# A mixer in two phases: input projection of the first 1024 tokens by seven block products, all recurrent chains after it

## The chip, the cores and the metric

The kernel runs on one core of a Trainium2 chip. Its time is the device time of one execution in microseconds; of several runs the median stands. PE is the matrix engine, DVE the vector engine, ACT the scalar engine, POOL the engine called GpSimd, SP the engine that issues most DMAs. DMAs run beside all of them.

## The reference

One layer over 2048 tokens of 1024 features, in fp32:

```
mod = silu(c) @ w_ada + b_ada             # six vectors: shift, scale, gate of mixer and feed-forward
p   = adaln(x, shift_m, scale_m) @ w_in   # 1024 -> 3592: gate_b, gate_c, h_conv, q, k, v, z, a, bt
ya  = rms_norm(gate_b * conv3(gate_c * h_conv))            # 512 wide, groups of 64
q, k, v = silu(conv4(q, k, v)); q, k normalized            # 4 heads of 128
o   = gated delta rule(q, k, v, g(a), beta(bt))            # a state per head, carried from token to token
yb  = rms_norm(o) * silu(z)
x   = x + gate_m * (concat(ya, yb) @ w_out)
x   = x + gate_f * ((silu(h @ w_gate) * (h @ w_up)) @ w_down)   # h = adaln(x, shift_f, scale_f)
out = adaln(x, shift_o, scale_o)
```

The delta rule goes in chunks: within a chunk a triangular system is solved; between chunks a state of 128 by 128 per head is carried, so chunk j+1 cannot begin before chunk j has updated the state. The convolutions are causal, three or four taps along the tokens.

## The kernel before

Dense products are made in fp32 accuracy from three matmuls: every operand is cut in a high part (a rounding on ACT, L389 for weights) and a low part (a difference on DVE, L391), and high times high, high times low and low times high are added in PSUM (`dmm`, L322).

The mixer takes the tokens in four blocks of 512. For each block the normalized rows are transposed to feature-major, scaled, shifted and split (`hTh`, `hTl`). Then 28 strips of 128 columns of w_in follow, 8 x 3 = 24 matmuls each: k, q, v and z of four heads, then four times gate_c, h_conv and gate_b. Sixteen narrow matmuls give a and bt. Behind each k, q and v strip stands its convolution on DVE (L1246, L1248) and a SiLU on ACT. Last comes the output projection, 8 strips of w_out, 192 matmuls for a block, whose result times gate_m is added to x and written to DRAM (`x1d`).

Beside the strips run the chains of the same block, written as generators: `head_chain` (decay and beta, the kk products, the triangular solve of diagonal pieces on DVE, L1041 and L1043, with a trip over DRAM before L1058), `level_chain` (products that join the pieces, L1082 to L1117), `q_chain`, `v_chain`, `chunk_chain` (L1182 to L1213: four matmul groups a chunk, each with a DVE step behind it), `out_chain` (norm, transposes at L1231, the pieces of yb at L1238) and `mix_chain` (the branch ya, with a reciprocal of 128x512 on DVE at L1321). A yield names what the next piece waits for. Every third dense matmul calls `tick`, which lets those generators go on whose next piece a planner (`Clock`, with estimated costs) holds to be ready. The order on PE, DVE, ACT and POOL is then fixed as the planner saw it. Each engine works through its list in that order.

Work in the background (`bg`) advances one step with each strip's weights: sums over w_ada (`mod_gen`), eight steps of 128x1024 on DVE at L469 for each vector; gate_m in block 0, the two vectors of the feed-forward norm in block 1, gate_f in block 2. The norm of x before the feed-forward (`second_norm`) runs one block behind. The feed-forward comes after and uses seven block products already.

## Time and profile before

| what | value |
|---|---|
| time, median of 3 runs | 2402.55 us (2399.51 to 2403.01) |
| the profiled execution | 2403.85 us, span 2402.1 us |
| PE / DVE / ACT / POOL busy | 2341.1 / 1788.3 / 1051.7 / 571.4 us |
| mixer (until the last output matmuls) | about 0 to 1055 us |
| DMA, mean over the span | 142 GB/s |

The page's parts are read in this order: busy shares and the 40 slices, then the chain that ended last, then windows over the mixer's stages, and last the chain of waits in one block with DVE's order of time beside it. Where PE's list holds a row that waits for another engine, everything behind it on PE waits too, even if it is ready.

### The profile page before, as it was taken

How to read it: one execution, taken by the hardware profiler on the slowest of the kernel's cores; microseconds unless marked ns; L12 is line 12 of the kernel's file. 1: busy time of each engine (PE TensorE's matmuls, PEld its weight loads, DVE VectorE, ACT ScalarE, POOL GpSimd, SP SyncE). 2: the span in 40 equal slices, each digit the busy share in tenths (PEclk: the TensorE clock that was granted, in tenths of full speed). 3: DMA queues.
4: the chain of work that ended last, by engine and by line, in shares of the span. 5: the costliest groups of instructions: out<-in, count | busy, mean ns of one | idle time of the engine just before them, and what ended most of it. 6: DMA issues, size and time to landing. Idle time of an engine off the chain costs nothing.

```text
span 2402.1 us, 31013 instructions
## 1 busy us (share of the span) xinstructions
PE 2341.1 (97%) x11317; PEld 1939.5 (81%) x11317; DVE 1788.3 (74%) x2673; ACT 1051.7 (44%) x1790; POOL 571.4 (24%) x643
## 2 busy tenths in 40 slices
PE   6999999999999999999999999999999999999998
PEld 5788888887888788887778888878888877887786
DVE  5988889775987678787556556875656569878888
ACT  3644664344544473366433334433333323322345
POOL 0340344033513161211000000000000036434447
PEclk9999999999999999999999999999999999999999
DMA  7443565535463445156664334753433374333433
GB/s 252 123 118 89 171 189 165 147 106 166 136 167 115 126 135 145 47 168 174 209 185 119 101 106 117 251 162 88 128 97 110 101 241 163 106 123 119 136 129 151
DMA packets 401136, 341.20 MB, mean 142 GB/s; under 512 B 39811, under 2 KB 343180, under 8 KB 400918
## 3 DMA queue, kind: packets, MB, share of 16 engines
q1 hardware_dynamic: 399430, 336.75, 45.9%
q0 software_dynamic: 1152, 2.10, 0.6%
q8 instruction: 89, 1.46, 0.2%
q14 instruction: 65, 0.53, 0.1%
q10 hardware_dynamic: 400, 0.36, 0.0%
HBM read 265.74 MB, written 75.51 MB: 142 GB/s over the span
## 4 chain that ended last, share of the span: by engine, by line
PE 66%; DVE 16%; DMA 7%; ACT 4%; issue 4%; POOL 2%; SPq 0%; ACTq 0%; DVEq 0%; POOLq 0%
PE pd L322 41%; PE pm L322 17%; DVE wlo L391 3%; DVE cv L1248 2%; DVE acc L1822 1%; DMA wraw<-in_w_in_dram 1%; ACT whi L389 1%; DMA y<-xT 1%; DVE wraw L469 1%; POOL wraw L1751 1%; DVE cv L1246 1%; PE pm L1082 1%; DMA A12d<-y 1%; DMA acc<-x 1%; PE pm L1090 1%
## 5 line engine op out<-in xcount | busy, mean ns | idle before, releaser
L389 ACT CAST whi<-wraw 128x1024 fp32r<-128x1024 f32 x286 | 299.7, 1050 | 404.5 <-PE pd L322 174.5
L391 DVE TENSOR_TENSOR wlo<-wraw,whi 128x1024 fp32r<-128x1024 f32 x286 | 361.9, 1266 | 98.4 <-ACT whi L389 94.2
L322 PE MATMUL pd<-hTh,whi 128*128 128x512 f32 x888 | 359.3, 406 | 0.6 <-ACT hTh L573 0.6
L322 PE MATMUL pd<-hTl,whi 128*128 128x512 f32 x888 | 346.9, 391 | 0.6 <-DVE hTl L574 0.6
L322 PE MATMUL pd<-hTh,wlo 128*128 128x512 f32 x888 | 347.2, 391 | 0.0
L322 PEld LDWEIGHTS pd<-hTh,wlo 128*128 128x128 f32 x888 | 166.8, 188 | 36.5 <-issue 0.3
L322 PEld LDWEIGHTS pd<-hTh,whi 128*128 128x128 f32 x888 | 167.3, 188 | 32.2 <-ACT hTh L573 1.0
L322 PEld LDWEIGHTS pd<-hTl,whi 128*128 128x128 f32 x888 | 167.6, 189 | 30.9 <-DVE hTl L574 1.1
L1616 POOL TENSOR_TENSOR wraw<-wraw 128x1024 f32<-128x1024 f32 x2 | 4.9, 2466 | 782.2 <-DMA wraw<-in_w_down_dram 773.8
L1564 DVE TENSOR_TENSOR sg<-sg,pd 128x512 f32<-128x512 f32 x44 | 30.2, 686 | 169.8 <-PE pd L322 169.8
L1822 DVE TENSOR_TENSOR acc<-acc,pd 128x512 f32<-128x512 f32 x192 | 127.4, 679 | 25.9 <-PE pd L322 24.3
L1702 ACT CAST xh<-ra 128x640 fp32r<-128x640 f32 (+1 forms) x85 | 60.4, 722 | 183.8 <-PE pm L322 134.6
L1248 DVE SCALAR_TENSOR_TENSOR cv<-pd,pcb,cv 128x511 f32<-128x511 f32 (+2 forms) x173 | 129.3, 748 | 5.2
L1711 POOL TENSOR_TENSOR xl<-ra,xh 128x640 fp32r<-128x640 f32 (+1 forms) x37 | 62.9, 1699 | 144.7 <-ACT xh L1702 144.7
L1822 DVE TENSOR_TENSOR acc<-acc,pm 128x512 f32<-128x512 f32 x120 | 81.7, 681 | 18.5 <-PE pm L322 18.1
L322 PE MATMUL pd<-whi,ym 128*128 128x512 f32 x256 | 84.8, 396 | 0.0
L1751 POOL TENSOR_TENSOR wraw<-wraw 128x512 f32<-128x512 f32 x40 | 70.0, 1772 | 46.9 <-DMA wraw<-in_w_down_dram 46.9
L322 PE MATMUL pd<-A22h,whi 128*128 128x512 f32 x176 | 70.4, 400 | 5.6 <-DVE sg L1564 5.6
L322 PE MATMUL pm<-S4h,whi 128*128 128x512 f32 x176 | 68.6, 390 | 1.3 <-ACT sg L1558 1.3
L322 PE MATMUL pd<-A22l,whi 128*128 128x512 f32 x176 | 69.7, 396 | 0.0
L322 PE MATMUL pd<-A22h,wlo 128*128 128x512 f32 x176 | 69.6, 395 | 0.0
L322 PE MATMUL pd<-S2h,whi 128*128 128x512 f32 x176 | 68.6, 390 | 1.0 <-ACT whi L389 1.0
(466 smaller groups left out, 6226.7 us busy)
## 6 DMA issues: line engine op xcount, KB each, us to landing
wraw<-in_w_in_dram SPq DMA_DIRECT2D x112, 512.0 KB
wraw<-in_w_gate_up_dram SPq DMA_DIRECT2D x88, 512.0 KB
ra<-act SPq DMA_DIRECT2D x80, 448.0 KB
wraw<-in_w_out_dram SPq DMA_DIRECT2D x40, 512.0 KB
act<-S SPq DMA_DIRECT2D x80, 256.0 KB
act<-act SPq DMA_DIRECT2D x68, 256.0 KB
wraw<-in_w_ada_dram SPq DMA_DIRECT2D x32, 512.0 KB
wraw<-in_w_down_dram SPq DMA_DIRECT2D x22, 512.0 KB
```

The costliest lines, as they stand in the source:

```text
L322: mm(*args, **kw)
L389: nc.scalar.copy(hi, raw)
L391: (lo_engines.popleft() if lo_engines else nc.vector).tensor_sub(lo, raw, hi.bitcast(F32))
L469: nc.vector.scalar_tensor_tensor(acc, raw, cs[:, k:k + 1], acc, op0=ALU.mult, op1=ALU.add)
L1082: mm(py[:, j * P:(j + 1) * P], Mm[h][:, j, :], T[h][:, j, :], start=True, stop=True)
L1090: mm(pz[:, j * P:(j + 1) * P], Y[h][:, j, :], Xs[h][:, j, :], start=True, stop=True)
L1248: nc.vector.scalar_tensor_tensor(cv[:, n - t:], u[:, :BLK - n + t], taps[t], cv[:, n - t:], op0=ALU.mult, op1=ALU.add)
L1564: nc.vector.tensor_add(s5[i], s5[i], a[i])
L1702: nc.scalar.copy(hi, raw[:, c0:c1, :])
L1711: eng.tensor_sub(lo, raw, hi.bitcast(F32))
L1751: nc.gpsimd.tensor_mul(r[:, hs], r[:, hs], gate_f[:, hs])
L1822: nc.vector.tensor_add(accs[s, u][:, ns], accs[s, u][:, ns], ps)
```

## The change

The mixer's work is ordered anew, in two phases.

Phase 1 computes the input projection of blocks 0 and 1 (1024 tokens) alone. The strips are taken in 14 pairs; a pair is a 2x2 block product (two strips of columns, two blocks of tokens, both halves of the 1024 features), made with seven products of sums in place of eight, 12 matmuls each: 84 matmuls for a pair where four strips of 24 took 96. The sums of inputs (A11, A12, S2, S1, S3, S4, A22) are built once; those of the weights (T1 to T4) for each pair, on DVE. Results are convolved, and k, q, v, z, ya and a, bt of both blocks are written to DRAM. Rows of x are copied to x1d by DMA, and rows of blocks 2 and 3 are normalized and transposed to DRAM (`norm_rows`). The sums for gate_m and for the two vectors of the feed-forward norm are made in phase 1; that for gate_f is moved to the feed-forward.

Phase 2 has four stages: strips 0 to 13 of block 2 beside the chain of block 0, strips 14 to 27 of block 2 beside block 1's, strips 0 to 11 of block 3 beside block 2's, strips 12 to 27 of block 3 beside its own. Each stage ends with the output projection of the block whose chain it held. Chains read k, q, v, z and (blocks 0 to 2) ya from DRAM; the next block's chain is started ahead of the output projection. Results are added to x1d by a DMA from POOL that accumulates. The last tap of each convolution goes to ACT.

```diff
+    YA_LAST = 2, 3, 0, 1
     def out_groups(b):
-        if b:
-            return [[(n, kp, range(CH)) for kp in KPS] for n in range(2)]
...
+        return [[(n, kp, range(CH)) for kp in (YA_LAST if n and b + 1 < NB else KPS)] for n in range(2)]
+    STRIPS = [(n, h) for n in "kqvz" for h in range(NH)] + [(n, m) for m in range(4) for n in ("gc", "hc", "gb")]
+    STAGES = (2, 0, 14), (2, 14, 28), (3, 0, 12), (3, 12, 28)
...
+    def prep_strips(pool, raw, W, x=None):
+        g, u = raw
+        b11, b21, b12, b22 = g[:, 0:4, :], g[:, 4:8, :], u[:, 0:4, :], u[:, 4:8, :]
...
+        nc.vector.tensor_sub(t3, b22, b12)
+        nc.vector.tensor_sub(b11, b12, b11)
+        nc.vector.tensor_sub(b12, b22, b11)
+        nc.vector.tensor_sub(b21, b21, b12)
...
+    def product(ps, w, a, start):
+        (wh, wl, k0), (ah, al) = w, a
+        for k in range(4):
+            first = dict(start=start and k == 0, skip_group_check=not start)
+            dmm(ps, wh[:, k0 + k, :], ah[:, k, :], stop=False, **first)
+            first["start"] = False
+            dmm(ps, wh[:, k0 + k, :], al[:, k, :], stop=False, **first)
+            dmm(ps, wl[:, k0 + k, :], ah[:, k, :], stop=k == 3, **first)
...
+        def rest(p, a, nxt=None):
+            w, (X, Y) = Ws.pop(p), PAIRS[p]
+            product(a, w["T2"], up("S2"), False)
...
+            if nxt:
+                hT.extend(ra.tile([P, KD, BLK], F32R, name=n) for n in ("r0", "r1"))
+                spawn(build_h(2), 1)
...
+            product(c_, w["T1"], up("S1"), True)
...
+            product(a, w["T3"], up("S3"), False)
...
+            product(c_, w["B22"], up("S4"), False)
...
+            product(a, w["T4"], up("A22"), False)
...
+        bg.append(mod_gen(w_ada, 2 * D, lambda acc: to_row(acc, b_ada[:, 2 * D:3 * D], row_dram(gate_md))))
+        bg.append(mod_gen(w_ada, 4 * D, lambda acc: to_col(acc, col["b_cf"], Gf, col["g_ffn"])))
+        bg.append(mod_gen(w_ada, 3 * D, lambda acc: to_col(acc, col["b_sf"], Sf)))
+        def back():
+            yield from half_two()
+            while bg:
+                step(bg)
+                yield clock.pe + 4.0
...
+        for p in range(NP):
+            last = p == NP - 1
+            if p == EARLY:
+                spawn(back(), 1)
...
+            if last:
+                while bg:
+                    step(bg)
+                drain()
...
+            rest(p, a, nxt if last else None)
...
             def conv(cv, u, taps, back):
-                nc.vector.tensor_scalar_mul(cv, u, taps[n])
+            nc.scalar.activation(cv, u, AF.Identity, scale=taps[n])
...
+        B = start_block(0, None)
+        for b, (src, s0, s1) in enumerate(STAGES):
+            if s0 == 0:
+                while src not in built:
+                    tick(True)
+                project_ab(src)
+            for s in STRIPS[s0:s1]:
+                dense_strip(src, s, B)
+            prev = B
+            if b + 1 < NB:
+                B = start_block(b + 1, prev)
+            if b == 1:
+                spawn(build_h(3), 1)
+            output(b, prev)
...
-                    if b + 1 < NB:
-                        nc.gpsimd.tensor_add(yo, yo, xr)
-                        nc.sync.dma_start(x1d[row][:, ns], yo)
-                    else:
-                        nc.gpsimd.dma_start(x1d[row][:, ns], yo, accum_op=ALU.add)
+                    nc.gpsimd.dma_start(x1d[b * CH + t][:, ns], yo, accum_op=ALU.add)
```

How the order moves is shown at three places. First PE, at the levels and first chunks of a chain. Before, in block 2 (L1107 and L1115 are the two products of the last level, L322 is the projection):

```order
L1107 MATMUL pm<-lv,ym 64x64 x16
L322 MATMUL pd<-hTh,whi 128x512
L322 MATMUL pd<-hTl,whi 128x512
L322 MATMUL pd<-hTh,wlo 128x512
L1115 MATMUL pm<-X,lv 64x64 x16
```

Of the change, in stage 0 (block 0's chain; L1459 and L1467 are the same two products, L1553 to L1563 a chunk, L1541 and L1544 its products with the state):

```order
L1459 MATMUL pm<-lv,ym 64x64 x16
L1467 MATMUL pm<-X,lv 64x64 x16
L1553 MATMUL pm<-vt,X 128x128 x4
L1561 MATMUL pm<-ch,kd 128x128 x4
L1563 MATMUL pm<-ch,E 128x128 x4
L1541 MATMUL pm<-state,kq 128x128 x4
L1544 MATMUL pm<-state,kq 128x128 x4
L1553 MATMUL pm<-ch,X 128x128 x4
```

Before, projection matmuls stand between the chain's groups; now, behind the 14 strips of the stage, the groups of the chain stand next to each other.

Second DVE, at the end of the triangular solve of the same chain in stage 0 (L1393 and L1395 are its steps; L1317 is the reciprocal for beta in the head of the next block, whose first matmuls on PE, L1281, stand right behind the stage's last strip):

```order
L1395 TENSOR_TENSOR yal<-yal,lv 128x4x14
L1317 RECIPROCAL beta<-beta 128x16
L1393 TENSOR_TENSOR lv<-yal 128x45
L1395 TENSOR_TENSOR yal<-yal,lv 128x3x15
L1393 TENSOR_TENSOR lv<-yal 128x30
L1395 TENSOR_TENSOR yal<-yal,lv 128x2x15
L1393 TENSOR_TENSOR lv<-yal 128x16
L1395 TENSOR_TENSOR yal<-yal,lv 128x16
```

Before, the solve's steps stood among convolutions and low parts of the same block; now a small step of the next block's head stands in front of the last three pairs.

Third DVE at the end of phase 1 (L467 is a step of a modulation sum, L951 a tap of a convolution, L486 the end of the sum for the shift of the feed-forward norm, L997 the first add of the last pair, L1129 the low part of block 2's rows):

```order
L465 TENSOR_SCALAR y<-y,cs 128x1024
L488 SCALAR_TENSOR_TENSOR Gf<-Gf,pca 128x8
L387 TENSOR_TENSOR wlo<-wraw,whi 128x1024
L951 SCALAR_TENSOR_TENSOR cv<-u,pcb,cv 128x512 x6
L467 SCALAR_TENSOR_TENSOR y<-y,cs 128x1024
...
L467 SCALAR_TENSOR_TENSOR y<-y,cs 128x1024 x4
L486 TENSOR_TENSOR Sf<-pm,pca 128x8
L997 TENSOR_TENSOR u<-u,pm 128x512
L387 TENSOR_TENSOR wlo<-wraw,whi 128x1024
L1129 TENSOR_TENSOR r_2952<-y,r_2951 128x1024 x2
```

These steps stood one by one beside single strips of block 1; now the last sum stands in one piece ahead of the last pair.

More of the change, by code (lines that the diff above doesn't have):

```diff
@@ new lines, in work_off, with u_tile, conv_u @@
+        def work_off():
+            while prep or posts:
+                work()
+        def u_tile():
+            return lu.tile([P, BLK + 4], F32, name="u", bufs=6)
+        def conv_u(cv, u, taps):
+            n = len(taps) - 1
+            nc.scalar.activation(cv, u[:, 4:], AF.Identity, scale=taps[n])
+            yield
+            for t in range(n - 1, -1, -1):
+                c0 = 4 - n + t
+                nc.vector.scalar_tensor_tensor(cv, u[:, c0:c0 + BLK], taps[t], cv, op0=ALU.mult, op1=ALU.add)
@@ new lines, in layer_kernel @@
+        split_next(nxt)
+        work_off()
+        drain()
+        early.close()
+        rb = pool(rctx, "rb2", "right", reuse_waits="tile")
+        lb = pool(actx, "lb2", "left", reuse_waits="tile")
+        ap_ = Areas(a=(ra, ("kq", "kd", "vt", "zs")), b=(rb, ("lv", "E", "Dg", "X", "ch", "state")),
+                    c=(lb, ("ym", "gate_m", "yah", "yal")), d=(ls, SMALL + TWICE))
+        temps[:] = wr, "wraw", 4
+        clock.pinned = True
+        room.update(lv=NLV, cv=NCV, ch=NCHN)
@@ new lines, in halo_terms @@
+        def halo_terms(sums, raw, taps):
+            k, n = raw.shape[1:]
+            taps = taps.rearrange("p (t m) -> p t m", m=k)
+            part = ap_.tile([P, k, n], F32, name="et")
+            for i in range(n):
+                tap = taps[:, i, :].unsqueeze(2).to_broadcast([P, k, n - i])
+                nc.gpsimd.tensor_mul(part[:, :, i:] if i else sums, raw[:, :, i:], tap)
+                if i:
+                    nc.gpsimd.tensor_add(sums[:, :, :n - i], sums[:, :, :n - i], part[:, :, i:])
@@ L906, in t16 @@
             def t16(name):
[L907 removed]
+                return small([P, CH, NH], name)
             def brd(v):
@@ L1362, in layer_kernel, with to_feed_forward, output @@
+        def to_feed_forward():
+            drain()
+            clock.pinned = mixing[0] = False
+            rctx.close()
+            spawn(first_sums(A), 1)
+        def output(b, B):
+            done, ybs = B.done, B.ybs
             for g, group in enumerate(out_groups(b)):
```

763 lines of the change are left out of this document (502 added, 261 removed).

## The prediction

> **What bounds the kernel now.** I read the page first: shares of busy time and the chain of work that ended last.
>
> ```profile
> PE 2341.1 (97%) x11317; PEld 1939.5 (81%) x11317; DVE 1788.3 (74%) x2673; ACT 1051.7 (44%) x1790; POOL 571.4 (24%) x643
> DVE  5988889775987678787556556875656569878888
> PE 66%; DVE 16%; DMA 7%; ACT 4%; issue 4%; POOL 2%; SPq 0%; ACTq 0%; DVEq 0%; POOLq 0%
> ```
>
> PE is the bound, and its waiting is small. DVE is second, and its slices are fullest (8 or 9 tenths) in the first fifth of the span. The table by stage says where PE stands still (columns: window, its length, busy us of PE, PEld, DVE, ACT, POOL with counts, granted clock, DMA share, GB/s).
>
> ```profile
> 0.00:25.00 25.00, 12.40 (x57) 12.10 (x58) 5.57 (x14) 11.57 (x17) 4.05 (x16) 1.00 0.93 302
> 25.00:50.00 25.00, 18.87 (x83) 15.04 (x83) 20.91 (x40) 10.82 (x18) 0.32 (x1) 0.86 0.80 259
> 75.00:100.00 25.00, 25.00 (x105) 20.44 (x104) 24.64 (x36) 18.83 (x21) 11.57 (x12) 0.93 0.57 155
> 100.00:125.00 25.00, 24.79 (x129) 20.64 (x128) 24.51 (x42) 15.14 (x38) 6.16 (x6) 1.00 0.50 143
> 75.00:1055.00 980.00, 972.34 (x5314) 816.89 (x5313) 793.17 (x1312) 492.37 (x963) 310.20 (x414) 1.00 0.47 135
> 449.00:454.60 5.60, 2.72 (x14) 1.90 (x13) 5.18 (x7) 1.56 (x2) 0.00 (x0) 1.00 0.61 157
> 454.60:458.00 3.40, 3.40 (x19) 3.40 (x18) 3.30 (x7) 3.11 (x4) 0.00 (x0) 0.50 0.94 270
> ```
>
> From 75 to 1055 us, the mixer's four blocks, PE idles 980.00 - 972.34 = 7.7 us. The last two rows show the price of a pause: half idle for 5.6 us, PE then runs 3.4 us at clock 0.50 and loses half of it, 1.7 us. One more such stretch lies in the window from 75 to 100 us (0.93 of 25 us is one of 3.4 us at half), so 7.7 + 3.4 = 11 us of the mixer are waiting in all.
>
> Why so little, although a chain of dependent steps runs in every block? The chain of waits in block 2 shows it (start us, duration us, what):
>
> ```profile
> 672.28 2.78 PE pd L322 x12
> 691.04 21.14 PE pd L322 x93
> 713.34 3.57 PE pm L1082 x32
> 716.91 0.69 PE pd L322 x3
> 717.60 3.57 PE pm L1090 x32
> 721.87 0.56 PE pm L1099 x8
> 724.80 2.00 PE pm L1107 x32
> 727.70 2.00 PE pm L1115 x32
> 729.70 1.59 PE pd L322 x6
> 731.28 0.89 PE pm L1182 x8
> 733.07 1.38 PE pd L322 x6
> 734.45 0.89 PE pm L1196 x8
> 736.71 0.89 PE pm L1204 x8
> 737.60 0.89 PE pm L1206 x8
> 739.19 0.89 PE pm L1182 x8
> 770.00 0.89 PE pm L1206 x8
> 777.74 0.44 PE pm L1231 x4
> ```
>
> Wherever the chain hands over to DVE, ACT or a DMA, projection matmuls (pd L322) fill PE. One of them costs 21.14 / 93 = 0.227 us. The chain itself is slow: the next rows, DVE's order of time, give its ends.
>
> ```profile
> 696.63 0.17 DVE L1043 TENSOR_TENSOR yal<-yal,lv 128x16 f32<-128x16 f32 x1
> 704.04 2.69 DVE L1058 TENSOR_TENSOR X<-Dg,ck 128x256 f32<-128x256 f32 x4 [0.42 <-DMA Dg<-dx]
> 778.08 1.23 DVE L391 TENSOR_TENSOR wlo<-wraw,whi 128x1024 fp32r<-128x1024 f32 x1 [2.81 <-ACT whi L389]
> 780.63 0.69 DVE L1238 TENSOR_TENSOR ym<-pm,ym 128x512 fp32r<-128x512 f32 x1 [0.65 <-ACT ym L1237]
> ```
>
> From the end of the solve (696.80) to the last piece of yb (781.32) it takes 84.5 us, of which PE works for the chain about a third.
>
> **The change part by part.** *Removed.* Fourteen pairs of strips at 84 matmuls instead of 96: 14 x 12 = 168 matmuls fewer, x 0.227 = **-38.1 us**, all on PE, the bound. This is the whole gain. Beside it the 11 us of the old mixer's waiting go: **-11**.
>
> *The start.* The first shift and scale rest on w_ada loads, as before; behind them now stand the first strips of four pairs and then the second halves of both tables, with x some 12 MB in all. At the 0.28 MB/us of the first two windows they land by 45 to 50 us, and only then can the second product of a pair begin. Against 0 us if the four first products cover it, and 12 us if ACT's splits pace all later sums, I take **+5**.
>
> *Phase 1 on DVE.* These groups of DVE operations carry it (75 to 1050 us; mean ns):
>
> ```profile
> L391 DVE TENSOR_TENSOR wlo<-wraw,whi 128x1024 fp32r<-128x1024 f32 x143 | 186.2, 1303 | 50.1 <-ACT whi L389 49.9
> L1321 DVE RECIPROCAL cv<-cv 128x512 f32<-128x512 f32 x15 | 50.2, 3348 | 13.7 <-ACT cv L1320 13.6
> L1248 DVE SCALAR_TENSOR_TENSOR cv<-pd,pcb,cv 128x511 f32<-128x511 f32 x62 | 46.4, 748 | 1.7
> L469 DVE SCALAR_TENSOR_TENSOR wraw<-wraw,cs 128x1024 f32<-128x1024 f32 x28 | 40.3, 1440 | 3.0 <-DMA wraw<-in_w_ada_dram 3.0
> L1339 DVE TENSOR_TENSOR pd<-pd,cv 128x512 f32<-128x512 f32 x16 | 11.1, 692 | 5.3 <-PE pd L322 5.3
> ```
>
> A pair of k, q or v strips needs three low parts of weights (3 x 1.30), four differences of half strips and three adds from PSUM (7 x 0.69), and twelve taps on four outputs (12 x 0.75): 17.7 us of DVE against 84 x 0.227 = 19.1 us of PE. That fits, until the three modulation sums that moved here come in at 1.44 us a step: by the order two or three stand in each of pairs 8 to 11, which makes 20.0 to 22.0 us. PE waits 1 to 2 us in each: **+5** (0 to 10; the window 100 to 125 us shows DVE at 24.5 of 25 us with PE hardly late).
>
> *The end of phase 1.* The last pair may go on only when all three sums are done. Between the adds of its neighbour and its own stand eight steps at 1.44, four of them in a row, low parts, nine taps and then the next block's splits: by the order 33.9 us of DVE rows, against 84 + 16 matmuls, 22.7 us of PE. The difference is 11 us, and behind it block 2's rows are still to be scaled and split before the first strip of phase 2. I take **+15** (5 to 30).
>
> *Phase 2.* The moved piece is the chain. Before, 28 strips (28 x 24 x 0.227 = 152 us) stood beside each block's chain; now 14, 14, 12 and 16. Let me follow stage 0 from the end of its last strip. In the order the transposes of the next block's head (L1281) stand right behind the strips, and DVE has the reciprocal of that head's beta ahead of the last three steps of block 0's solve. So the solve ends 5 to 6 us after the strips. Then:
> - solve to first level matmul: 713.34 - 696.80 = 16.5 us in block 2; with reciprocals of 3.35 us between, 17.
> - levels, 713.34 to 731.28: 17.9 us with 5.7 us of projection inside; the handovers remain, so 17.
> - chunks: 731.28 to 739.19 is 7.9 us for one. The first of all has no state product, 5 us; three more make 23.7.
> - from the last L1206 (770.89) to the last yb: 10.4 us in block 2; a low part of weights (778.08) stood 1.1 us ahead of its scaling, so 9.3.
>
> That is 5.5 + 17 + 17 + 28.7 + 9.3 = 77.5 us. What can PE do meanwhile? By the order only 42 output matmuls (9.5 us) and the chain's own: levels 12.3, chunks 16, transposes and the mixing branch's sums 5; together 43. Exposed: **+34** (18 if every handover is at its floor, 45 if reciprocals on DVE delay it).
>
> Stage 1 has 14 strips too, but its chain began earlier: the first chunk stands 11 matmuls ahead of the strips' end. Four chunks and the tail are 31.6 - 2.5 + 9.3 = 38.4 us against 9.5 + 17.6 of PE: 11, with next head's and mixing operations on DVE between them **+14** (5 to 24). In stage 2, with 12 strips, the first level matmul stands at the strips' end: 17 + 31.6 + 9.3 = 58 against 9.5 + 12.3 + 19.6 + 2: 14, and for the same reason **+18** (7 to 28). Stage 3 has 16 strips, and its chain is covered as before. Beside these, in stage 0 twelve convolutions (4 us of DVE a strip with its weights) and the chain's own DVE work fill about all of 76 us of strips: **+5** (0 to 12). Small waits elsewhere, loads of spilled tiles among them, about half of the old 11: **+6**.
>
> *Clock.* Pauses of several us now come in a row. At 1.7 us for each half-rate stretch, as the rows at 449 to 458 us show, and four of them on the path: **+6** (0 to 20).
>
> The edits that I cost at nothing: the accumulating DMA into x1 in place of a load and an add on POOL (nobody waits for x1 until the norm some us later; else 2 us for each block), the 16 copies of x rows (8 MB in phase 1, where DMA's share was 0.5), and the conv's last tap on ACT (44% busy), which relieves DVE by 0.74 us a strip.
>
> Sum: -38.1 - 11 + 5 + 5 + 15 + 34 + 14 + 18 + 5 + 6 + 6 = +59. The profiled execution took 2403.85 us (its span is 2402.1, the rest lies around it), 1.3 above the median of 2402.55; against that median the sum gives 2461. I forecast **2461 us**: slower.
>
> **The rivals.**
> 1. *The chain passes at its floor.* With 18 + 5 + 7 in the stages, 5 at the end of phase 1, 4 of small waits and nothing else: -49 + 39 = -10, **2393 us**. For it: the planner that sets the order places other work where it sees a wait, and block 2's handovers are never seen unfilled, so they may be shorter than the filled rows. Against it: in the order nothing is left to fill with. It decides below 49 us of new waiting in all.
> 2. *Only the count moves* (2402.55 - 49): **2353 us**. The order's rows in stage 0 speak against it.
> 3. *Half rate through the stages.* Some 115 us of PE work (87 of chain, 28 of output) lie in stretches where PE is busy half the time, as it was at 449 us, just before the clock fell to 0.50. If about 35 us more of chain work pass at half rate, **2496 us**. The clock of 1.00 from 75 to 1055 us speaks only for full stretches. The Trainium skill, "TensorE: Matmul & The Clock Gate", Part 1, gives half rate after about one idle window of 3.4 us; by that rule a PE with pauses of 1 to 2 us would keep its clock, and this rival falls. The row at 449 us, where PE was busy for half of 5.6 us before the clock fell, leaves it a chance.
> 4. *DVE sets phase 1 and the stages* (start 12, pairs 10, end 25, stage 0's strips 10, stages 85, clock 10, small 8, less 49): +111, **2514 us**. The nines in DVE's early slices speak for it, the relieved tap against.
>
> **How the numbers follow.** Chances: the forecast 0.57, rival 1 0.17, rival 2 0.03, rival 3 0.11, rival 4 0.08, and 0.04 that the terms cancel to within 0.2% (about what a measurement of this kernel can tell from no change). So faster 0.20, same 0.04, slower 0.76. The range must take in most of rivals 1 and 3: 2390 to 2510; the forecast's own, from the terms' bounds taken half each, is 2428 to 2496.
>
> **What would show it.** After the strips of stages 0, 1 and 2 the windows should show PE 10 to 35 us short of full, with PE waits named by DVE and ACT at the level and chunk lines, and the clock under 1.00 in some. Phase 1 should show 267 us of products (14 x 84 x 0.227) and 20 to 30 us of waiting, the largest piece at its end with DVE full. The count of matmuls in the projection must fall by 168. PE gaps in the three stages summing to under 30 us would make the prediction wrong.

## The result, and the profile after

The changed kernel takes **2568.05 us** (median of 4 runs, 2563.88 to 2573.59) against 2401.03 us of the kernel before (4 runs, 2397.5 to 2403.01): ratio 1.0699, with an interval of 1.0674 to 1.0724. It is 7% slower. The direction was forecast, the size was not: 2461 us was predicted, with a range up to 2510.

The page of the changed kernel, its busy time and two rows of the 40 slices:

```profile
PE 2372.5 (92%) x11219; PEld 1958.8 (76%) x11219; DVE 1773.8 (69%) x2598; ACT 1097.3 (43%) x1897; POOL 620.4 (24%) x707
PE   7899977968997986999899999999999999999998
PEclk9899988969998998999999999999999999999999
```

PE fell from 97% to 92% of the span. Nearly all of the new holes lie in the first 20 slices, the mixer and the begin of the feed-forward, and the clock falls in most of the slices with holes. No other engine's share of the span grew by as much as half a per cent. The windows of the changed kernel place the holes (columns as in the prediction: window, its length, busy us of PE, PEld, DVE, ACT, POOL, granted clock, DMA share, GB/s):

```profile
0.00:150.00 150.00, 121.78 (x518) 101.17 (x519) 82.76 (x126) 78.19 (x122) 30.62 (x41) 0.93 0.65 212
150.00:350.00 200.00, 194.13 (x876) 156.31 (x875) 151.44 (x195) 109.80 (x163) 57.57 (x78) 1.00 0.54 162
350.00:425.00 75.00, 47.00 (x189) 35.99 (x188) 36.03 (x57) 27.46 (x41) 11.84 (x19) 0.77 0.62 197
425.00:500.00 75.00, 72.78 (x379) 61.18 (x379) 61.51 (x120) 48.57 (x111) 37.73 (x40) 1.00 0.45 130
500.00:642.00 142.00, 106.92 (x574) 90.63 (x573) 80.62 (x140) 42.39 (x90) 39.93 (x57) 0.82 0.29 79
642.00:750.00 108.00, 106.92 (x641) 90.98 (x640) 84.32 (x159) 65.28 (x142) 35.69 (x50) 1.00 0.61 171
750.00:845.00 95.00, 76.49 (x392) 63.82 (x391) 52.03 (x76) 27.90 (x64) 36.91 (x50) 0.91 0.38 103
845.00:925.00 80.00, 80.00 (x427) 66.43 (x426) 69.02 (x148) 50.10 (x119) 32.91 (x46) 1.00 0.71 195
925.00:1058.00 133.00, 99.52 (x567) 83.85 (x566) 73.93 (x106) 43.79 (x91) 34.85 (x49) 0.90 0.26 75
1058.00:1242.00 184.00, 182.80 (x1059) 156.51 (x1058) 147.98 (x245) 103.41 (x224) 55.52 (x80) 1.00 0.52 142
1242.00:2566.00 1324.00, 1284.18 (x5615) 1051.96 (x5613) 934.20 (x1235) 500.42 (x735) 246.82 (x202) 0.99 0.46 144
```

Rows 1 and 2 are phase 1; row 3 is its end and the first strips of phase 2. Each of stages 0, 1 and 2 is two rows: first the strips, where PE is full at clock 1.00, then the tail, where a fifth to a quarter of the time is idle and the clock is 0.82, 0.91 and 0.90. Stage 3, with 16 strips, is full. The last row is the feed-forward, 1324 us, where the kernel before has this:

```profile
150.00:1092.00 942.00, 934.08 (x5115) 784.76 (x5114) 754.28 (x1245) 475.87 (x923) 279.18 (x383) 1.00 0.47 137
1092.00:2402.00 1310.00, 1279.95 (x5611) 1049.85 (x5610) 919.69 (x1223) 499.90 (x732) 248.37 (x202) 1.00 0.46 142
```

What PE waited for in the changed kernel (us in total, times, the longest; the first rows of the list):

```profile
PE pd L318 <- ACT ym L1595: 26.0, 12, 7.4
PE pd L318 <- ACT whi L385: 14.0, 2, 8.0
PE pm L1281 <- DMA cv<-ab: 13.9, 1, 13.9
PE pd L318 <- ACT yah L1630: 13.1, 3, 6.1
PE pm L1321 <- DVE g L1310: 13.1, 2, 11.5
PE pm L481 <- DVE y L467: 11.9, 1, 11.9
...
PE pm L1553 <- DVE ch L1547: 10.2, 8, 5.7
```

Four kinds of waits from the mixer stand in it: the chain's own handovers (ym L1595 is the last piece of yb, L1553 is in the chunks), the mixing branch (yah L1630), the next block's head (L1281, L1321), and the last modulation sum of phase 1 (L481).

**The account.** To put one figure on each stretch, I take for every matmul the time to the next one's start and subtract what is usual for its kind (the 20th percentile of the whole trace); the sum is PE's *loss*, idle time and half rate together. Even a full stretch shows some: 4.8 us in the 184 us of stage 3, 2.6%. That floor is taken off in the table.

| where | predicted | measured |
|---|---|---|
| products of the input projection | -38.1 | -38.1 (168 matmuls fewer) |
| waiting of the old mixer behind its start | -11 | -12.3 |
| start (0 to 150 us) | +5 | +25.3: 17.0 more of narrow sums, 8.3 of loss |
| phase 1 behind it, and its end (150 to 426 us) | +20 | +40.0 |
| stages 0 to 2 (426 to 1058 us) | +71 | +124.6 |
| small waits, clock | +12 | in the rows above |
| other PE work, difference of the floors | 0 | +10.4 |
| feed-forward | 0 | +14.4 |
| sum | +59 | +164.3 (span 2566.4 against 2402.1) |

The total is measured; its split is not exact. If the matmuls are grouped into kinds in another way, single rows move by a few us (the old mixer's 12.3 becomes 7.9 when they are grouped by the length of the moving operand alone), and the row of other PE work takes up the difference.

Half rate is inside these figures: counted over matmuls that took 1.6 to 2.4 times their usual interval, it is about 50 us in the changed kernel and 15 before. The granted clock of the traces, taken over the time in which PE was busy, gives 53 and 11.

**Stage 0, row by row.** DVE in order of time, from the end of the solve to the last piece of yb (start us, duration us):

```profile
517.21 0.25 DVE L1317 RECIPROCAL beta<-beta 128x16 f32<-128x16 f32 x1 [1.58 <-POOL beta L1316]
...
518.46 0.17 DVE L1395 TENSOR_TENSOR yal<-yal,lv 128x16 f32<-128x16 f32 x1
...
525.92 0.71 DVE L1428 STREAM_TRANSPOSE lv<-X 128x512 f32<-128x512 f32 x1 [2.51 <-POOL X L1410]
526.56 3.31 DVE L1628 RECIPROCAL cv<-cv 128x512 f32<-128x512 f32 x1
...
530.57 0.76 DVE L1410 TENSOR_TENSOR X<-Dg,ck 128x256 f32<-128x256 f32 x2
...
531.95 3.35 DVE L1628 RECIPROCAL cv<-cv 128x512 f32<-128x512 f32 x1
...
536.06 0.76 DVE L1410 TENSOR_TENSOR X<-Dg,ck 128x256 f32<-128x256 f32 x2
...
537.44 1.89 DVE L1428 STREAM_TRANSPOSE lv<-X 128x512 f32<-128x512 f32 x3
...
605.36 0.69 DVE L1596 TENSOR_TENSOR ym<-pm,ym 128x512 fp32r<-128x512 f32 x1 [0.65 <-ACT ym L1595]
```

And PE in the same stretch:

```profile
510.06 0.42 PE L1281 MATMUL pm<-ck,cv 16*128 16x16 f32 x4
521.94 0.58 PE L1321 MATMUL pm<-g,ck 128*128 128x16 f32 x2 [11.46 <-DVE g L1310]
...
531.36 0.79 PE L318 MATMUL pd<-whi,yah 128*128 128x512 f32 x1 [6.09 <-ACT yah L1630]
...
536.85 0.79 PE L318 MATMUL pd<-whi,yah 128*128 128x512 f32 x1 [3.85 <-ACT yah L1630]
...
544.32 3.73 PE L1434 MATMUL pm<-lv,ym 128*128 128x128 f32 x32
...
561.80 2.07 PE L1553 MATMUL pm<-vt,X 128*128 128x128 f32 x8
```

The strips end at 510.1, the solve at 518.6, the first level matmul (L1434) starts at 544.3, the first chunk at 561.8, the last piece of yb is done at 606.0. In steps: 8.6 (5.5 predicted), 25.7 (17), 17.5 (17), 44.2 (38.0); 96.0 us for 77.5. The largest miss is the second. There two of the mixing branch's reciprocals, 3.3 us each, stand on DVE between the pieces of X (L1410) that the levels wait for. On PE output matmuls of that branch stand ahead of L1434 and wait for the same reciprocals through `yah`; L1434's last input left DVE at 539.3, PE reached it at 544.3.

### The profile page after: what moved, and what is told of

Its sections match the earlier page's. It is cut to its first block, busy times and chain, and to the rows that moved or that the text cites. A ratio compares the mean times of both kernels' runs of the same rounds, so it can differ in the third digit from the quotient of the medians.

```text
span 2566.4 us, 31216 instructions
## 1 busy us (share of the span) xinstructions
PE 2372.5 (92%) x11219; PEld 1958.8 (76%) x11219; DVE 1773.8 (69%) x2598; ACT 1097.3 (43%) x1897; POOL 620.4 (24%) x707
## 3 DMA queue, kind: packets, MB, share of 16 engines
q8 instruction: 88, 1.44, 0.2%
## 5 line engine op out<-in xcount | busy, mean ns | idle before, releaser
L385 ACT CAST whi<-wraw 128x1024 fp32r<-128x1024 f32 x264 | 276.1, 1049 | 379.6 <-PE pd L318 185.0
L387 DVE TENSOR_TENSOR wlo<-wraw,whi 128x1024 fp32r<-128x1024 f32 x264 | 327.1, 1241 | 135.9 <-ACT whi L385 134.3
L318 PE MATMUL pd<-r,whi 128*128 128x512 f32 x1008 | 343.6, 405 | 3.6 <-ACT u L991 2.6
L318 PEld LDWEIGHTS pd<-r,whi 128*128 128x128 f32 x1008 | 192.2, 191 | 44.2 <-ACT u L991 4.0
L318 PE MATMUL pd<-r,wlo 128*128 128x512 f32 x504 | 199.1, 395 | 0.0
L318 PEld LDWEIGHTS pd<-r,wlo 128*128 128x128 f32 x504 | 96.6, 192 | 16.6
L318 PE MATMUL pd<-S3l,t3h 128*128 128x512 f32 x232 | 91.2, 393 | 0.0
L318 PE MATMUL pm<-S4l,whi 128*128 128x512 f32 x232 | 90.9, 392 | 0.0
L318 PE MATMUL pm<-S4h,wlo 128*128 128x512 f32 x232 | 90.5, 390 | 0.0
L318 PEld LDWEIGHTS pd<-whi,ym 128*128 128x128 f32 x256 | 51.6, 202 | 40.9 <-ACT ym L1595 29.3
```

Source lines behind the costliest of these rows:

```text
L318: mm(*args, **kw)
L385: nc.scalar.copy(hi, raw)
L387: (lo_engines.popleft() if lo_engines else nc.vector).tensor_sub(lo, raw, hi.bitcast(F32))
```

## The experiments

All edits are to the changed kernel unless "before" is named. Each was run beside the kernel before on the same chip, which took 2396 to 2403 us. Loss figures are those of the account, floor included (changed kernel: stages 0, 1, 2 lose 58.9, 31.8, 50.4). One run decides nothing under some 5 us: the changed kernel's own four runs spread over 10 us.

### What holds up the stages

**The next block's head.** L1321 waits 11.5 us in stage 0, and everything behind it on PE waits too. The edit lets the head begin only when the chain before it is far enough:

```diff
             def head_chain():
+                yield from after("cc")
                 yield from take("cv", 1)
```

> The next block's head (L1281 to L1325) may start only when this block's chunk chain is done. Theory A, other chains' pieces stand in front of the levels and chunks in the in-order lists: PE's wait of 11.5 us at L1321 in stage 0 and the head's pieces in stage 2 go, the stretches after the strips lose some 20 us less, the next chains begin later by up to 10 us in all; 2568 falls to 2545 to 2558. Theory B, the chain is bare and nothing is left to fill it: the stretches keep their length, and the next solve comes later by a head's 15 us; 2565 to 2600.

Measured: 2568.05 us, the same as the changed kernel to the last digit. The longest wait at that row fell from 11.5 to 5.1 us, but all waits there add up to 14.0 us in three places, where it was 13.1 in two:

```profile
PE pm L1322 <- DVE g L1311: 14.0, 3, 5.1
```

(The inserted line shifts line numbers by one.) The stages lose 57.2, 33.1 and 46.5, four us less in all, and the first level matmul of stage 0 still comes 21.4 us after the solve (25.7 in the changed kernel). So the wait of 11.5 us stood in front of others, and taking away more than half of it did not shorten the kernel. Theory A, that the head in front of the chain sets the stage, finds no support; as the head still waits in other places, the run does not exclude it for those.

**Reciprocals of the mixing branch.**

```diff
                 nc.scalar.activation(sy, ps, AF.Sqrt, scale=1.0 / 64, bias=epsc)
-                nc.vector.reciprocal(sy, sy)
                 nc.vector.scalar_tensor_tensor(cv, cv, col["g_conv"][:, m:m + 1], sy, op0=ALU.mult, op1=ALU.mult)
```

> The mixing branch leaves out its reciprocal (3.35 us of DVE, 16 times), so ya is scaled wrongly. Theory D, the mixing branch's work on DVE holds up the levels after the solve: from the solve's end to the first level matmul in stages 0 to 2 it takes 13 us in place of 25, total 2530 to 2545. Theory B: DVE has time there; total 2558 to 2566.

Measured: 2524.94 us, -43. The stages lose 43.1, 20.8 and 36.9: 15.8, 11.0 and 13.5 less. Four reciprocals of 3.35 us are 13.4 us of DVE in a stage, so over the three stages (40.3 us for 40.2) they were paid one to one. The end of the solve and the first level matmul of stage 0 in this run:

```profile
518.11 0.17 DVE L1395 TENSOR_TENSOR yal<-yal,lv 128x16 f32<-128x16 f32 x1
```

```profile
535.49 3.74 PE L1434 MATMUL pm<-lv,ym 128*128 128x128 f32 x32
```

This step takes 17.2 us in place of 25.7. The 13 us of theory D were not reached in this step, but the whole gain of 43 us is larger than the 23 to 38 that it expected.

**The branch's norm as a whole** (square, split, sums on PE, root, reciprocal, scaling):

```diff
                     yield cv,
-                yield from take("lv", 2)
-                sy = cv_tile([P, BLK])
-                nc.scalar.activation(sy, cv, AF.Square)
...
-                nc.vector.reciprocal(sy, sy)
-                nc.vector.scalar_tensor_tensor(cv, cv, col["g_conv"][:, m:m + 1], sy, op0=ALU.mult, op1=ALU.mult)
                 nc.scalar.copy(yah[:, m, :], cv)
```

> The mixing branch leaves out its whole norm (square, split, sums on PE, root, reciprocal, scaling); ya is only split, so its values are wrong. Theory D, this branch stands in front of the levels: stages 0 to 2, which lost 59, 32 and 50 us on PE, lose under 20 each; total 2470 to 2500, well below the 2525 without the reciprocal alone. Theory B, the chain without fill is the rest: total 2505 to 2520, each stage still loses 15 to 40 us.

Measured: 2496.37 us, -72. The stages lose 40.2, 16.5 and 28.8, 85.5 in all. The total lies in theory D's range, the losses left in stages 0 and 2 in theory B's. What is left belongs to the chain without the branch; less the floor (2.6% of 571 us, 15) it is 70.5. In stage 0 the three steps from the solve's end (to the first level matmul, to the first chunk, to the last piece of yb) take 12.4, 12.2 and 42.1 us; in the changed kernel they take 25.7, 17.5 and 44.2.

**More work for PE in the tails.** If the chain's latency sets a stage's end, matmuls added beside it cost nothing. The first group of products of each output projection in stages 0 to 2 is made twice in one kernel (72 matmuls more, 16.3 us at 0.227) and four times in another (216 more, 49.0 us); the edit of the first:

```diff
-                        for k in range(2):
+                        for r, k in enumerate((0, 1, 0, 1) if i == 0 and n == 0 and b + 1 < NB else range(2)):
...
-                            dmm(ps, yh, wh[:, k, :], start=(i == 0 and k == 0), stop=False)
+                            dmm(ps, yh, wh[:, k, :], start=(i == 0 and r == 0), stop=False)
```

> In blocks 0 to 2 the first 24 output matmuls are made twice and added (ya's first half counts double there): 72 dense matmuls more, 16.3 us of PE. All theories of a late chain: they disappear in the waits, 0 to 4 us longer (2566 to 2574). If PE's own work set these stretches: 2580 to 2586.

> As the run with 24 output matmuls doubled in blocks 0 to 2, but made four times: 216 dense matmuls more, 49.0 us of PE (ya's first half counts four times). Theory B, the stages' ends have nothing to fill the chain with: the three ends lost 59, 32 and 50 us, so most of it disappears; total 2555 to 2580, and the excess of PE in the stages falls by 35 us or more. If DVE or the loads behind these matmuls set the ends, not the dependent steps: 2595 to 2617.

Measured: 2560.73 us (-7) and 2553.74 us (-14). With 49 us more of matmuls the kernel is 14 us *faster*; by the traces the three stages are 10 us shorter. With 16 us more they are 3 us shorter, which single runs cannot tell from no change; that these matmuls cost nothing is shown. The window of stage 0's tail, in the changed kernel (quoted above: PE 106.92 of 142 us, clock 0.82), with 72 matmuls and with 216:

```profile
500.00:642.00 142.00, 107.17 (x616) 88.87 (x615) 81.13 (x139) 43.88 (x98) 42.24 (x60) 0.89 0.31 80
```

```profile
500.00:642.00 142.00, 115.53 (x651) 97.33 (x650) 81.14 (x140) 42.30 (x91) 41.05 (x58) 0.88 0.30 79
```

42 more matmuls in the first, yet hardly more busy time: the others ran at the higher clock. This is theory B's sign: the tails are as long as the chain is, whatever PE has to do beside it. That the chain became a little shorter because its own matmuls ran at the higher clock fits these rows, but no run shows it alone.

### What holds up phase 1

**The order of the SP queue.** SP's list holds the loads of a chain between larger loads and the stores of k, q, v and z, and takes them one after the other. The loads of a and bt (`ab`) and of ya go to POOL's queue, the four kinds of store to ACT's:

```diff
-                nc.sync.dma_start(abr, abd[b])
+                nc.gpsimd.dma_start(abr, abd[b])
...
-                    nc.sync.dma_start(cv, yad[b][m])
+                    nc.gpsimd.dma_start(cv, yad[b][m])
...
-                nc.sync.dma_start(spill[n][b][i], cv)
+                nc.scalar.dma_start(spill[n][b][i], cv)
...
-                nc.sync.dma_start(zd[b][i], cv)
+                nc.scalar.dma_start(zd[b][i], cv)
```

> The loads of a, bt and of ya go out on POOL's queue, and the stages' results of k, q, v and z are written from ACT's queue, so that SP's list holds no store that waits for a convolution in front of a load. Theory C, SP's queue makes the chains late: PE's wait of 13.9 us at the first L1281 falls to 3, and stage 2's wait for ya (14.5 us of SP standing still at the stores of v) goes; 2568 falls by 15 to 25, to 2543 to 2553. Theories A and B: less than 8 us.

What stood there in the changed kernel, SP's list in order of time at the start of phase 2, and in stage 2 (start us, us that the entry held the queue):

```profile
397.82 2.48 SPq L1263 DMA_DIRECT2D kq<-kT  x4
400.35 6.14 SPq L1263 DMA_DIRECT2D kq<-qT  x4
...
407.01 1.96 SPq L1271 DMA_DIRECT2D zs<-z  x3
...
411.51 0.44 SPq L1277 DMA_DIRECT2D cv<-ab  x1
...
927.25 14.51 SPq L1692 DMA_DIRECT2D v<-cv  x3
941.85 0.38 SPq L1277 DMA_DIRECT2D cv<-ab  x1
```

PE waited 13.9 us, until 416.8, for the little load of `ab`, which went out 14 us after the loads of k began: it stood behind loads of k, q, z and weights, not behind stores. In stage 2 three stores held the same load back for 14.5 us. Measured: 2543.12 us, -25. The stretch from 371 to 426 us loses 7.6 in place of 22.5; the 13.9 us at L1281 are gone. The stages hardly move (55.7, 33.5, 45.7, together 6 less), so the wait in stage 2 was covered or replaced. This points to the moved load of `ab` as what gained; the two edits were not run apart. The rest, 4 us, lies in stage 3 and the feed-forward, within the spread of single runs.

The Trainium skill, "DMA: Bandwidth & Descriptors", Rules for kernel authors, says that spreading DMAs over the issuing engines does not help bandwidth and saves only the issuer's time. That bandwidth was not the question the rows agree: the stretch of the wait moved 197 GB/s, the prediction's first window 302. The saving was 25 us here all the same, and its largest part (15 us) comes from a small load that the order of one list put behind large ones.

**The pace of the background work.** In the changed kernel the last sum of phase 1 lands in one piece ahead of the last pair:

```profile
369.43 1.28 DVE L467 SCALAR_TENSOR_TENSOR y<-y,cs 128x1024 f32<-128x1024 f32 x1 [1.76 <-DMA y<-in_w_ada_dram]
...
375.34 1.29 DVE L467 SCALAR_TENSOR_TENSOR y<-y,cs 128x1024 f32<-128x1024 f32 x1 [1.73 <-DMA y<-in_w_ada_dram]
```

Between the two rows stands one more step. Each takes 1.28 us and waits 1.6 to 1.8 more for its load; the prediction had 1.44 and no wait. Stepping it more often:

```diff
             while bg:
                 step(bg)
-                yield clock.pe + 4.0
+                yield clock.pe + 2.0
```

> In phase 1 a step of the modulation sums is due every 2 us of the planner's time instead of every 4, so that all three are done before the last pair. Theory E, the wait of 12 us at the last sum (L481, with half-rate clock behind it) comes from where the steps were put: the stretch from 350 to 400 us loses 12 to 16 us less, total 2552 to 2558, with 0 to 4 us given back in the pairs before, where DVE is nearly full. If DVE's whole work in phase 1 sets its end: within 4 us of 2568.

Measured: 2543.82 us, -24. The wait at L481 is gone, and from 150 us to phase 2's first strips the loss is 31.0 in place of 47.1: 16 of the 24 us. Another 5 lie in stage 0, the rest within the spread. The gain is larger than the 10 to 16 us that were expected.

**The start.** Two edits. The second halves of the shift and scale tables are not loaded but copied from the first; and the first half of shift is summed on DVE instead of PE:

```diff
-        late = [list(ada_raw(c0, 1)) for c0 in (D, 0)]
...
-        ada_scale(col_sums(accs[0], 4), K1)
-        ada_shift(col_sums(accs[1], 4), K1)
+        nc.vector.tensor_copy(Gm[:, K1], Gm[:, K0])
+        nc.vector.tensor_copy(Sm[:, K1], Sm[:, K0])
```

> The second halves of the shift and scale tables aren't loaded or summed (4 MB of w_ada less at the start); the first halves stand in for them, so half the features are scaled wrongly. Theory F, the start waits for DMA: at 0.28 MB/us the second products begin 10 to 14 us earlier, total 2554 to 2560. If ACT's and DVE's work on the sums of inputs sets the start: 2562 to 2568.

```diff
-        sums = sums_pe(0)
+        sums = col_sums(sums_dve(ada_raw(0, 0)), 4)
```

> The first half of the shift table is summed on DVE (eight steps and four small matmuls) in place of PE (L842: 64 matmul rows of 0.213 us, 13.6 us). Theory G, PE itself is the bound of the first 40 us, by these narrow sums, without waiting for anything: the first product begins at about 38 us in place of 46, total 2558 to 2563. Theory F, loads set it: within 4 us of 2568.

Measured: 2556.78 us (-11) and 2563.47 us (-5). Without the second halves the start's loss is 28.6 in place of 38.2. With shift on DVE the first dense matmul comes at 37.8 us (46.3 in the changed kernel, 28.3 before) and 338 dense matmuls are done by 150 us (307; before 373), yet phase 2 begins only 4.7 us earlier, and the 5 us of the time are within what single runs spread. These rows of the changed kernel, then of the kernel before, show what PE does first (0 to 150 us; mean ns):

```profile
L842 PE MATMUL pm<-cs,kd 128*128 128x1 f32 x32 | 7.0, 353 | 0.1
...
L842 PE MATMUL pm<-cs,S3l 128*128 128x1 f32 x32 | 6.8, 339 | 0.0
```

```profile
L796 PE MATMUL pm<-cs,ym 128*128 128x1 f32 x48 | 10.4, 352 | 0.2 <-ACT cs L376 0.2
```

Four such groups of 32, 128 narrow sums instead of 48: 80 more, at 0.213 us from start to start, are 17.0 us of PE before the first strip can begin.

### What the moved pieces cost by themselves, in the kernel before

gate_f's sum in the feed-forward instead of block 2, and the convolution's tap on ACT:

```diff
-            if b == 2:
-                bg.append(mod_gen(w_ada, 5 * D, lambda acc: to_row(acc, b_ada[:, 5 * D:6 * D], row_dram(gate_fd))))
...
+    bg.append(mod_gen(w_ada, 5 * D, lambda acc: to_row(acc, b_ada[:, 5 * D:6 * D], row_dram(gate_fd))))
...
-            if hf:
+            if hf or not side:
                 bg_step()
```

> The kernel before, with one part of the change alone: the sum for gate_f is made in the feed-forward. Nine steps of 1.3 to 1.4 us of DVE move from block 2, where PE never waits, to the feed-forward, where DVE is at 55 to 65%. If this is part of the feed-forward's loss of 14 us: 2 to 5 us longer than before; if that is all the accumulating DMA and the clock: within 1 us.

```diff
-                nc.vector.tensor_scalar_mul(cv, u, taps[n])
+                nc.scalar.activation(cv, u, AF.Identity, scale=taps[n])
```

> The kernel before, with another part alone: the last tap of each convolution on ACT (64 operations of 0.74 us leave DVE, 64 of 0.69 go to ACT). DVE is full from 75 to 150 us only: 0 to 4 us shorter if PE's spacing there is DVE's, and no change if weights' loads or ACT set it; 1 to 3 us longer if ACT's table loads or its place ahead of the weights' high parts cost more.

Measured against 2401.58 us: 2407.01 us, ratio 1.0025 (1.0014 to 1.0037), and 2405.76 us, 1.0018 (1.0009 to 1.0027). Both came out 4 to 5 us longer. So did a third edit of the kernel before, reported below (2406.28 us), which has nothing to do with either; the 5 us may therefore not belong to the moved pieces. The profiled execution of the first is the fastest of its seven (2401.45 us) and shows a feed-forward of 1308.8 us, no longer than before, so its trace does not say where the median's 5 us lie.

The other way round, gate_f's sum goes back to phase 1, with the faster pace:

```diff
+        bg.append(mod_gen(w_ada, 5 * D, lambda acc: to_row(acc, b_ada[:, 5 * D:6 * D], row_dram(gate_fd))))
...
-                yield clock.pe + 4.0
+                yield clock.pe + 2.0
```

> The sum for gate_f is made in phase 1 again, behind the other three, with steps due every 2 us, and not in the feed-forward. Compare with the run with that pace alone (2543.8): if the moved sum is the feed-forward's loss, the feed-forward takes 1310 to 1314 us in place of 1323, and phase 1 some 8 to 15 us more (nine steps of DVE at 1.3 us near its end); if the loss is the wait at its begin (8 us behind a landing of the accumulating DMA): feed-forward 1319 to 1323.

Measured: 2558.72 us, 15 slower than the faster pace alone. The feed-forward takes 1316.4 us instead of 1322.6, between the two ranges; phase 1 loses 47.5 again in place of 31.0. So the sum may cost up to 6 us in the feed-forward, but this is not shown: in the other runs of the changed kernel, all with the sum there, the feed-forward took from 1318.6 to 1327.9 us, and in the profiled execution of the kernel before the moved sum added nothing to it.

Most of the 14 us stands at the feed-forward's first products. Its 263rd matmul starts 68.4 us behind its begin in the changed kernel and 58.5 before, 10 us later. PE waits 8.0 us there for weights on ACT (L385, second row of the list of waits), and part of what follows runs at half rate. ACT's list shows what it did meanwhile; first the changed kernel, then the kernel before:

```profile
1253.83 1.14 ACT L1836 CAST t3h<-T 128x512 fp32r<-128x512 f32 x2 [7.93 <-DMA x<-cv]
```

```profile
1096.80 1.23 ACT L1457 CAST t3h<-T 128x512 fp32r<-128x512 f32 x2 [0.79 <-DVE T L1447]
```

ACT's next cast, a part of the next weights, waits 7.93 us for the last accumulating DMA into x1, and the split of weights stands behind it. The kernel before writes its last block with the same accumulating DMA, and its cast has no such wait. So the accumulation by itself is not the cause; that the cast's new buffer lies where the DMA's source lay would fit, but is not shown. In every run of the changed kernel PE waits at this place (7 to 10 us), and none took the wait away.

### The repairs together

Queue, pace, and the root and reciprocal as one operation on ACT:

```diff
-                yield clock.pe + 4.0
+                yield clock.pe + 2.0
...
-                nc.scalar.activation(sy, ps, AF.Sqrt, scale=1.0 / 64, bias=epsc)
-                nc.vector.reciprocal(sy, sy)
+                nc.scalar.activation(sy, ps, AF.Abs_reciprocal_sqrt, scale=1.0 / 64, bias=epsc)
...
-                nc.sync.dma_start(abr, abd[b])
+                nc.gpsimd.dma_start(abr, abd[b])
...
-                nc.sync.dma_start(spill[n][b][i], cv)
+                nc.scalar.dma_start(spill[n][b][i], cv)
```

> Three mends of the change together, with the right result: loads and stores off SP's list as in the run with the queues, the modulation sums' steps due every 2 us as in that run, and the mixing branch's root and reciprocal replaced by one reciprocal root on ACT. If the three causes are separate places, their gains add: 25 + 24 + about 40, total 2476 to 2490. If they share a wait (the first gone, the next takes its place): 2500 to 2525. In either case above the kernel before, by 70 us or more: what is left is the chain without fill and the start.

The same operation alone in the kernel before, and the joint kernel with 216 matmuls more in the tails:

> The kernel before, with the reciprocal root on ACT in place of root on ACT and reciprocal on DVE (16 times, 3.35 us of DVE each). PE hardly waits for DVE there, so the same work that costs 13 us a stage after the change should be nearly free here: 0 to 5 us shorter than before.

> The three mends together, and the 216 dense matmuls more (49.0 us of PE; ya's first half counts four times). With queue, pace and reciprocal out of the way the stages still lost 100 us on PE; theory B: 2490 to 2510, the waits take the matmuls. If what is left there is not fillable: 2530 to 2543.

Measured: the joint kernel takes 2493.61 us against 2401.61, ratio 1.0382 (1.0354 to 1.041), 74 us below the changed kernel, between the two ranges expected. The three gains measured one by one add up to 92 (25, 24 and 43; the expectation had 40 for the last). By the ends of the stages in the traces, 9 of the missing 18 us lie before the end of stage 0, 2 in stage 2, and 7 in stage 3 and the feed-forward, where the single runs' gains of 0 to 3 us were within their spread. The end of phase 1 is full:

```profile
335.00:410.00 75.00, 73.75 (x338) 58.55 (x339) 58.17 (x89) 51.40 (x78) 32.75 (x39) 1.00 0.63 198
```

The stages still lose 43.7, 21.6 and 34.8: 100 us, 85 without the floor. In the kernel before the one operation in place of two gains nothing: 2406.28 us, ratio 1.0017 (1.0006 to 1.0029). With 216 matmuls more the joint kernel takes 2498.36 us, 5 more for 49 us of work; its stages lose 35.0, 6.0 and 17.3. So about 44 of its 85 us are room that PE's work would fill for nothing; the joint kernel's own four runs spread over 9 us. No version was faster than the kernel before.

## Why the prediction was wrong, point by point

**What held.** The direction; the 168 matmuls and 38.1 us; the old mixer's 11 us (8 to 12, by the grouping); stage 3 as covered as before. Two agreements are luck in part. The levels took 17.5 us for 17, but a third of that time lay at half rate, and without the branch they took 12.2. The chain without the mixing branch costs 70.5 us over three stages, where 34 + 14 + 18 + 5 = 71 was forecast (35, 12 and 24 by stage, floor off), but the forecast had mixing operations and full-DVE strips in it, and in stage 0 the steps were 12.4, 12.2 and 42.1 us where 17, 17 and 38.0 were forecast. The method, handover by handover against the PE work that is left, named the right stages.

**Stages: the mixing branch.** The step that failed is "solve to first level matmul ... with reciprocals of 3.35 us between, 17", and with it the choice of +34 from bounds whose upper end, 45, was written for "if reciprocals on DVE delay it". They did: the step took 25.7 us in stage 0, and 17.2 with the reciprocals left out. Without the branch's norm the stages lose 55.6 us less, of which the reciprocals alone make 40.3. The row for them (50.2 us in all) stood in the prediction. It was read as work with an engine that has time; in these tails, with no fill, the twelve reciprocals lengthened the stages by as much as they take (40.3 us for 40.2). That the bare chain and the branch do not simply add up was not tested.

**End of phase 1.** "I take +15" with 5 for the pairs: 40 us in place of 20. Of these, 16 belong to the placing of the last sum, whose steps come about 3.0 us apart, not 1.44, because each waits for its load. Another 15 are SP's list, which had no term: the prediction priced no queue, and the load of `ab` in front of the first chain is where it shows. The rest, some 9 us, was not separated. (In the sum for the pairs, two steps more make 20.6 us of DVE, not 20.0; this changes nothing.)

**Start.** +5 against 25. The transfer of second halves was sized (11 us at most by its removal); 17 us of narrow sums on PE itself were overlooked. They are in the code as 128 matmuls of one column, but no row of them was quoted or priced. Taking half of the 128 off PE, 13.7 us of its time, brought the first dense matmul 8.5 us forward and the kernel 5, so they are not all of it either; what else holds the first 46 us was not separated.

**Clock.** +6 against 35 to 42 (50 less 15; by the granted clock 53 less 11). Rival 3 had this mechanism and its size: it put 35 us of half rate on top of the forecast, with a chance of 0.11. Its 2496 us failed with the other terms. Part of the half rate goes when the tails are filled: with 216 matmuls more, it falls from 27.5 to 13.3 us in the stages.

**Feed-forward.** +14, not foreseen. Ten of it stand at the first products, behind ACT's wait for the landing of an accumulating DMA. The prediction costed this DMA at nothing, since "nobody waits for x1 until the norm some us later". Here it is no norm that waits but a cast of weights; and as the last block accumulated in the kernel before too, without that wait, the cause is open. The move of gate_f's sum was listed as a change but given no term; what it costs lies between 0 and 6 us. Neither this move nor the tap on ACT was a gain in the kernel before.

**Bounds.** Adding all upper ends gives -49 + 12 + 10 + 30 + 45 + 24 + 28 + 12 + 6 + 20 = +138, 2540 us; even these do not reach 2568. So the range failed from missing terms (SP's queue 15, narrow sums 17, feed-forward 14) as much as from choosing the lower half of known ones. Rival 4, DVE in phase 1 and the stages, came nearest in its sum (2514); rivals 1 and 2, which need the tails filled, were excluded by the first window.

**Still open.** Which waits take the joint kernel's missing 18 of 92 us; the wait at the begin of the feed-forward, untried; why each of three small edits of the kernel before costs it 4 to 5 us.

## What to carry to other kernels

Before taking work off the bounding engine, compare for each stage the work that is left beside a dependent chain with the chain's own length: where it is shorter, the removed work buys nothing, and every operation in front of a handover, free until then, is paid in full (the reciprocals: nothing in the kernel before, 13 us a stage after). Read the lists of all engines at a phase's boundary, the DMA issuer's too, for a small load behind large stores and loads. When terms have an upper end with a named cause, look whether that cause is in the order before taking the lower one.

## What the runs showed of the hardware

Adding 49.0 us of matmuls made the kernel 14 us faster, one run against four that spread over 10 us: the granted clock in stage 0's tail was 0.88 in place of 0.82. With 16.3 us more it was 0.89, and the time 7 us shorter, hardly more than single runs spread.

In one place the clock fell to half without any long pause. Windows in stage 0 of the changed kernel, over the levels:

```profile
552.70:555.20 2.50, 1.89 (x18) 1.35 (x19) 1.76 (x3) 1.28 (x4) 0.00 (x0) 1.00 0.67 180
555.20:558.50 3.30, 3.30 (x38) 3.16 (x38) 2.15 (x1) 1.97 (x5) 0.39 (x1) 0.62 0.10 28
558.50:561.80 3.30, 3.30 (x36) 3.18 (x32) 3.26 (x6) 0.98 (x2) 3.30 (x4) 0.50 0.00 0
```

From 552.7 us on PE runs 64x64 products with pauses of at most 0.63 us, and the clock falls from 1.00 to 0.50 between 555.2 and 558.5 us, while PE counts as fully busy. The Trainium skill, "TensorE: Matmul & The Clock Gate", Part 1, ties half rate to an idle window of about 3.4 us; the same part describes a second way, brief and frequent idling between groups of matmuls. These rows agree with the second and not with the first. Whether the short pauses or the small products cause it, no run told apart. Elsewhere in this stage the half rate does stand at a long wait: from 515 to 542 us the granted clock was 0.50, and L1321 had kept PE idle from 510.5 to 521.9.

Root and reciprocal as one ACT operation (`Abs_reciprocal_sqrt`) replace a 3.35 us DVE operation; in the kernel before, where that was covered, it gained nothing (2406.28 us against 2401.61).
